# Forming the z projection of a hybrid encoder layer as seven half-size products in front of the heads

## The chip, the cores and the metric

The kernel runs on one NeuronCore of a Trainium2 chip. The metric is the device time of one execution in microseconds. Three runs of the kernel before took 2490.58, 2490.86 and 2491.49 us. Traces come from one more, profiled execution.

## What is computed

One layer for 512 tokens of width 2048, in float32. The input is RMS-normalised to h and multiplied by one wide matrix:

```python
h = rmsnorm(x, g_pre)
qkv, z_a, b_raw, a_raw, glu_in, z_b, gate_logits = split(h @ w_in)   # 6144, 2048, 16, 16, 4096, 2048, 4096 columns
# A: gated DeltaNet over 16 heads of 128
o_a = gated_delta_chunked(q, k, v, g_log, beta)
o_a = rmsnorm(o_a, g_dn_out).reshape(B, S, 2048) * silu(z_a)
y_a = o_a @ w_br_a
# B: GLU, causal depthwise convolution of 31 taps, layer norm
u = silu(layernorm(conv31(glu(glu_in)) + b_dw)) * silu(z_b)
y_b = u @ w_br_b
gate_a, gate_b = split(sigmoid(gate_logits + b_gate))
x = x + rmsnorm((gate_a * y_a + gate_b * y_b) @ w_out, g_post)
x = x + rmsnorm(sigmoid(x @ w_ple_gate) * (p @ w_ple_proj), g_ple)
```

The change concerns z_a (called z below), z_b (zb) and the two gates. For z, h is a 512 x 2048 matrix and its weight a 2048 x 2048 one.

## The kernel before, in words

**Products.** Every operand of a large product is split into a high part in the rounded type fp32r and a low remainder, and three matmuls (high-high, high-low, low-high) accumulate in a PSUM bank. `hT` holds h transposed, channels on partitions, as 16 pairs of 128x512 tiles, written at L261 (ScalarE, high) and L262 (VectorE, low). `gemm_cm` (L168) makes one output tile of 128 channels by 512 tokens from one 128-column slice of a weight: 16 k-tiles x 3 matmuls of 128x128 by 128x512 (L181, L183, L185), 48 in all. Its weights come as two loads of 512 KB into `raw` (three buffers, L121 and L122). Each load gives two pieces, and a piece is split by a ScalarE copy (L127) and a VectorE subtraction (L128) into one of four `ring` buffers. Three pieces are kept ready ahead of TensorE (L131); a piece serves 12 matmuls.

**Order.** Tiles are queued as `jobs` and run in order. `tick` (L142) counts matmuls: after every matmul each active generator comes one nearer to its next step. So the heads (`group`, a step every 4 matmuls, L664), the depthwise convolutions (every 6), the layer norm (every 10, L867) and the mixing of the branches (every 6) are issued between the matmuls of the tiles. `finish` (L152) issues what is left of a generator at once. The framework that builds the program derives the waits from the data, and gives each engine an order of its own from dependencies, free buffers and the place in the program.

**Stages.** `load_x` (L223) loads x, makes the embedding product and hT. The beta and decay tile (L267) follows, then for each of eight pairs of heads six tiles for k, q and v, the start of `group(g)`, and two tiles for z (L665): z is evacuated by a Silu with channels on partitions (`evac_z`, L438) and kept in the pool `za`. `head_scan` (L445) ends with the RMS scale (L497), a transpose of the head's output by TensorE (L502) and a multiply by g_dn_out and z (L510), once z is there (L504). Then four gate_a tiles and a GLU pair finish the heads; branch A's product runs with the other gate_a tiles, 15 GLU pairs and, on GpSimd's queue, sums of blocks of `w_out` made by accumulating loads (`presum`, L759). The gates (`evac_gate`, L712, a Sigmoid) stay in SBUF, as `mixed` and `gate_b`. The layer norm (L806) runs beside the 16 zb tiles (L869, `evac_zb`, a Silu) and the first two gate_b tiles, and ends in a Silu of its own (L848). Branch B's 16 tiles run with the other 14 gate_b tiles (L952).

**The output product** (from L998) is already made as seven half-size products in place of eight, for each half of its columns, with tokens on partitions: the stationary operands are sums and differences of quarters of the transposed activations (A11, S1 to S4), the moving ones blocks of the weight or their sums. The output's quarters are combined from the products by VectorE. The embedding gate's product follows.

**Buffers.** `slots` (L92) is a pool of 21 tiles of 128x512, shared by nearly all passing data; `lop` and `s2` (L731) hold branch B's; `gps` has two PSUM banks.

Of the kernel before, what the change touches and what calls it, by code (L numbers as in the profile page):

```python
# [9 lines left out]
F32 = mybir.dt.float32  # L10
# [5 lines left out]
P = 128  # L16
# [66 lines left out]
def _body(ctx, tc, A, out):  # L83
# [26 lines left out]
    def vv(col, n=1):  # L110
        return vec[:, col:col + n]
# [27 lines left out]
    def spawn(gen, period, key=None):  # L139
        active.append([gen, period, period, key])  # L140
# [24 lines left out]
    def w_in_tile(t):  # L165
        return A["w_in"][t]
# [56 lines left out]
    def load_x():  # L223
        with tc.tile_pool(name="xin", bufs=1) as xin, tc.tile_pool(name="xps", bufs=6, space=PSUM) as xps:
# [3 lines left out]
            prep_src.extend(ba_src)  # L228
# [209 lines left out]
    def evac_z(h):  # L438
        def f(ps):
            z = hd.tile([P, T], F32, tag="za", name="za", bufs=3)  # L440
            nc.scalar.activation(z, ps, AF.Silu)
            hstate[h].update(z=z)
        return f

    def head_scan(g, hh, G):  # L445
# [4 lines left out]
        O = hd.tile([P, NTT, P], F32, tag="O", name="O", bufs=2)  # L450
        S = None
# [44 lines left out]
        for tt in range(NTT):  # L496
            nc.vector.tensor_scalar(O[:, tt, :], O[:, tt, :], rs2[:, tt:tt + 1], None, ALU.mult)  # L497
# [6 lines left out]
        while "z" not in st:  # L504
            yield
        oa = slots.tile([P, T], F32, tag="s", name="oa")
        oav = oa.rearrange("p (t x i) -> p t x i", x=2, i=64)
        zv = st["z"].rearrange("p (t x i) -> p t x i", x=2, i=64)
        for x in range(2):
            nc.vector.scalar_tensor_tensor(oav[:, :, x, :], po[:, :, 1 - x, :], vv(V_GDN), zv[:, :, x, :], ALU.mult, ALU.mult)  # L510
# [201 lines left out]
    def evac_gate(dst, i, col, pool=None):  # L712
        def f(ps):
            gt = (pool or slots).tile([P, T], F32, tag="s2" if pool else "s", name="gt")
            nc.scalar.activation(gt, ps, AF.Sigmoid, bias=vv(V_BG + col))
            dst[i] = gt
        return f

    def gate_a(i):
        gemm_cm(w_in_tile(GATE_TILE0 + i), hT, evac_gate(mixed, i, i))  # L720

    for i in range(4):
        gate_a(i)
# [31 lines left out]
    B11, B12, B22, B21 = range(4)  # L755
# [32 lines left out]
    gate_a(4)  # L788
    glu_pair(1)
    jobs.append(lambda: finish("oa"))  # L790
    jobs.append(lambda: spawn(presum(), 10, "presum"))
    nglu = 2
    for i in range(NK):
        gemm_cm(A["w_br_a"][i], oT, evac_ya(i))
        if i + 5 < NK:
            gate_a(i + 5)
        if nglu < NK:
            glu_pair(nglu)
            nglu += 1
# [6 lines left out]
    def layer_norm():  # L806
# [36 lines left out]
        nc.scalar.copy(rstd, prs)  # L843
        yield
        for i in range(NK):
            u = u_t[i]
            nc.vector.tensor_tensor(u, u, rstd, ALU.mult)
            nc.scalar.activation(u, u, AF.Silu, scale=vv(V_LNG + i), bias=vv(V_LNB + i))  # L848
            yield
            while zb[i] is None:  # L850
                yield
# [8 lines left out]
    def evac_zb(i):  # L860
        def f(ps):
            z = low(0, "zb", F32)
            nc.scalar.activation(z, ps, AF.Silu)
            zb[i] = z
        return f
# [21 lines left out]
    LO, HI = slice(0, 256), slice(256, 512)  # L887
# [54 lines left out]
    AHEAD = 5  # L942

    def gate_b_tile(i, pool):
        gemm_cm(w_in_tile(GATE_TILE0 + 16 + i), hT, evac_gate(gate_b, i, 16 + i, pool))

    gate_b_tile(order[0], None)
    gate_b_tile(order[1], None)
    jobs.append(finish)
    for n in range(2, AHEAD):  # L950
        gate_b_tile(order[n], s2)
    for n, i in enumerate(order):  # L952
        if n + AHEAD < NK:
            gate_b_tile(order[n + AHEAD], s2)
        elif n + AHEAD == NK:
            jobs.append(lambda: spawn(mix, 6, "mix"))
        gemm_cm(A["w_br_b"][i], uT, evac_yb(i))
# [7 lines left out]

# [32 lines left out]
    OPND = {"P1": "A11", "Q5": "S1", "P7": "S3", "P6": "S2", "P3": "S4", "P2": "A12", "Q4": "A22"}  # L998
# [143 lines left out]

    def stepper(gen, n=1):
        def f(k=None):
            for _ in range(n):
                next(gen, None)
        return f
# [220 lines left out]
```

## Time and profile before

| what | value |
|---|---|
| median of three runs | 2490.86 us |
| the profiled execution | 2490.88 us |
| its span, first to last instruction | 2489.1 us |
| TensorE busy | 2469.3 us (99%) |
| VectorE busy | 1639.5 us (66%) |
| ScalarE busy | 1055.6 us (42%) |
| GpSimd busy | 230.8 us (9%) |
| granted TensorE clock, mean | 0.999 of full |
| moved by DMA | 319.32 MB, mean 128 GB/s |

PE is TensorE's matmuls and PEld its weight loads, DVE is VectorE, ACT is ScalarE, POOL is GpSimd, SP is the engine that issues most DMAs; a q behind a name is that engine's instruction queue. L181 is line 181 of the kernel. `out<-in` names the tiles that an instruction writes and reads. Busy time adds up the durations of instructions, which overlap in part on TensorE and VectorE. A time in square brackets behind an instruction is how long its engine had been idle, and what released it.

### The profile page before, as it was taken

The page shows a single profiled execution, that of the slowest core. Times are in us where ns is not written, and L with a number is a line of the kernel's source. Part 1 is how long each engine was busy: PE and PEld are TensorE (multiplying, and loading weights), DVE is VectorE, ACT ScalarE, POOL GpSimd, SP SyncE. Part 2 cuts the span into 40 slices and gives each one's busy share as a digit, 9 for nine tenths or more (in the row PEclk, how much of TensorE's full clock was granted, in tenths as well). Part 3 has the DMA queues.
Part 4 walks back from the last instruction along what each step waited for, and adds up shares of the span by engine and source line. Part 5 has one row for each costly group of instructions (what it writes and reads, how often), then busy time and mean ns, then how long its engine had stood idle before and what let it go on. Part 6 is the DMA issues. An engine that isn't in the chain of part 4 may idle for free.

```text
span 2489.1 us, 32807 instructions
## 1 busy us (share of the span) xinstructions
PE 2469.3 (99%) x12202; PEld 2037.7 (82%) x12202; DVE 1639.5 (66%) x3076; ACT 1055.6 (42%) x2083; POOL 230.8 (9%) x295
## 2 busy tenths in 40 slices
PE   9999999999999999999999999999999999999998
PEld 7888888888888888888888888887888888788886
DVE  6776767767676776887786869937423336667644
ACT  6555455565645555322222222235422224444532
POOL 0100000000000001313313200012000000000000
PEclk9999999999999999999999999999999999999999
DMA  7322222222122223857848632432232232664642
GB/s 262 119 94 73 90 76 84 83 77 90 64 94 81 77 90 93 241 157 199 220 141 224 194 110 98 155 117 95 95 101 94 95 101 94 212 235 162 202 169 77
DMA packets 101728, 319.32 MB, mean 128 GB/s; under 512 B 11968, under 2 KB 12224, under 8 KB 101568
## 3 DMA queue, kind: packets, MB, share of 16 engines
q1 hardware_dynamic: 83520, 273.18, 33.0%
q0 software_dynamic: 16896, 41.95, 6.9%
q10 hardware_dynamic: 1152, 2.10, 0.3%
q8 instruction: 95, 1.56, 0.3%
q14 instruction: 65, 0.53, 0.1%
HBM read 285.73 MB, written 31.46 MB: 127 GB/s over the span
## 4 chain that ended last, share of the span: by engine, by line
PE 97%; DVE 1%; issue 1%; ACT 0%; POOL 0%; DMA 0%; SPq 0%; DVEq 0%; POOLq 0%; ACTq 0%
PE g L183 26%; PE g L185 26%; PE g L181 25%; PE f L1052 2%; PE f L1053 2%; PE f L1051 2%; PE f L1223 2%; PE f L1222 2%; PE f L1221 2%; PE psB L467 1%; PE psS L473 1%; PE psA L461 1%; PE pg L568 1%; PE f L1300 0%; PE f L1298 0%
## 5 line engine op out<-in xcount | busy, mean ns | idle before, releaser
L185 PE MATMUL g<-hh,w 128*128 128x512 f32 x2320 | 914.9, 394 | 1.6 <-DVE w L128 1.6
L183 PE MATMUL g<-hl,w 128*128 128x512 f32 x2320 | 915.5, 395 | 0.0
L181 PE MATMUL g<-hh,w 128*128 128x512 f32 x2320 | 912.8, 393 | 0.0
L127 ACT CAST w<-raw 128x512 fp32r<-128x512 f32 x780 | 478.3, 619 | 862.8 <-PE g L185 761.5
L128 DVE TENSOR_TENSOR w<-raw,w 128x512 fp32r<-128x512 f32 x780 | 552.0, 712 | 433.7 <-ACT w L127 431.8
L185 PEld LDWEIGHTS g<-hh,w 128*128 128x128 f32 x2320 | 436.2, 188 | 88.9 <-DVE w L128 4.7
L183 PEld LDWEIGHTS g<-hl,w 128*128 128x128 f32 x2320 | 436.1, 188 | 86.8 <-issue 1.6
L181 PEld LDWEIGHTS g<-hh,w 128*128 128x128 f32 x2320 | 436.3, 188 | 84.4 <-issue 0.2
L688 DVE SCALAR_TENSOR_TENSOR uc<-sg,vec,uc 128x511 f32<-128x511 f32 (+14 forms) x480 | 351.3, 734 | 14.0 <-ACT uc L685 3.9
L409 DVE SCALAR_TENSOR_TENSOR cv<-g,vec,cv 128x511 f32<-128x511 f32 x144 | 106.5, 740 | 31.2 <-ACT cv L407 30.8
L181 PE MATMUL g<-oh,w 128*128 128x512 f32 x256 | 99.6, 389 | 0.0
L183 PE MATMUL g<-ol,w 128*128 128x512 f32 x256 | 99.6, 389 | 0.0
L185 PE MATMUL g<-oh,w 128*128 128x512 f32 x256 | 99.6, 389 | 0.0
L181 PE MATMUL g<-uh,w 128*128 128x512 f32 x256 | 99.6, 389 | 0.0
L183 PE MATMUL g<-ul,w 128*128 128x512 f32 x256 | 99.6, 389 | 0.0
L185 PE MATMUL g<-uh,w 128*128 128x512 f32 x256 | 99.6, 389 | 0.0
L603 DVE TENSOR_TENSOR prod<-UT,VT 128x2 f32<-128x2 f32 (+30 forms) x248 | 87.3, 352 | 6.6
L767 POOL DMA_DIRECT2D wsum<-in_w_out x96 | 75.2, 839 | 72.1 <-issue 22.3
L1052 PE MATMUL f<-wsp,oph 128*128 128x512 f32 x192 | 75.4, 393 | 0.1
L1051 PE MATMUL f<-wsp,oph 128*128 128x512 f32 x192 | 75.5, 394 | 0.0
L1221 PE MATMUL f<-w,xh 128*128 128x512 f32 x192 | 75.4, 393 | 0.0
L1053 PE MATMUL f<-wsp,opl 128*128 128x512 f32 x192 | 75.2, 392 | 0.0
(303 smaller groups left out, 2742.3 us busy)
## 6 DMA issues: line engine op xcount, KB each, us to landing
raw<-in_w_in SPq DMA_DIRECT2D x290, 512.0 KB, 3.3
wsum<-in_w_out POOLq DMA_DIRECT2D x96, 256.0 KB, 5.3
raw<-in_w_ple_gate SPq DMA_DIRECT2D x40, 512.0 KB, 3.4
raw<-in_w_br_a SPq DMA_DIRECT2D x32, 512.0 KB, 3.7
wo_sums<-wsum POOLq DMA_DIRECT2D x64, 256.0 KB, 3.9
raw<-in_w_br_b SPq DMA_DIRECT2D x32, 512.0 KB, 3.3
rw<-wo_sums SPq DMA_DIRECT2D x20, 512.0 KB, 4.1
rw<-in_w_out SPq DMA_DIRECT2D x13, 512.0 KB, 5.0
```

The costliest lines, as they stand in the source:

```text
L127: nc.scalar.copy(hi, rq)
L128: nc.vector.tensor_tensor(lo, rq, hi.bitcast(F32), ALU.subtract)
L181: mm(ps, wh, rh, start=(k == 0), stop=False)
L183: mm(ps, wh, rl, start=False, stop=False)
L185: mm(ps, wl, rh, start=False, stop=(k == NK - 1))
L409: nc.vector.scalar_tensor_tensor(y[:, s:], ps[:, 0:T - s], vv(w0 + 3 - s), y[:, s:], ALU.mult, ALU.add)
L603: pin(nc.vector.tensor_tensor(pv_, um, vm, ALU.mult))
L688: nc.vector.scalar_tensor_tensor(y[:, s:], u[:, 0:T - s], vv(w0 + TAPS - 1 - s), y[:, s:], ALU.mult, ALU.add)
L1051: mm(ps, lh, wh[:, c], start=kk == 0, stop=False)
L1052: mm(ps, lh, wl[:, c], start=False, stop=False)
L1053: mm(ps, ll, wh[:, c], start=False, stop=kk == 7)
L1221: mm(ps[tt], lh, wh, start=k == 0, stop=False)
```

## The change

The z tiles between the heads go. In front of the heads there is a new phase, `z_phase`. Four gate tiles (`FILL`) run first, and beside them, every 4 matmuls, a step of `form`: it adds hT's high and low parts and builds and splits S1 to S4. Then, for each of the two halves of z's columns (`jp`), three runs of products: P1 and Q5, then P6, P7 and P3, then P2 and Q4. Each product has four quarters q of the k range with two weight pieces of 128x512 each; a piece serves 6 matmuls. Blocks of the z weight are loaded in pieces of 512 KB, 3 of 5 into `raw`, 2 of 5 into slots; T1 (B11 + B12) and B12 + B22 are formed by VectorE, and T2 and T4 by accumulating loads on GpSimd's queue onto T1 (B22, then B21). The results have tokens on partitions; a Silu on ScalarE and two stores put each into DRAM, by head, with the halves of 64 tokens swapped as the heads hold them. `head_scan` loads its z, multiplies it in at the RMS scale, and the evacuation of the transpose becomes a ScalarE copy scaled by g_dn_out.

All other gate tiles and the zb tiles are made in the places that are free (`rest`, in the order gate_a 4 to 15, zb 0 to 15, gate_b 0 to 15): two behind each pair of heads, five around the first two GLU pairs, eleven in branch A's product, and the last twelve beside the layer norm. Each is stored to DRAM and loaded again three tiles ahead of its use. The layer norm's period goes from 10 to 8 matmuls; the mixing is spawned with a period of 10 before the seventh tile of branch B, instead of 6 before the twelfth. The beta tile comes behind the z phase.

```diff
-    ba_src = [w_in_tile(BA_TILE)[0], w_in_tile(BA_TILE)[1]]
+    z_dram = dram.tile([NH, P, NTT, P], F32, name="z_dram")
+    g_dram = dram.tile([2 * NK, P, T], F32, name="g_dram")
+    zb_dram = dram.tile([NK, P, T], F32, name="zb_dram")
+    def gate_tile(i, src=True):
+        def f(ps):
+            t = slots.tile([P, T], F32, tag="s", name="gt")
+            nc.scalar.activation(t, ps, AF.Sigmoid, bias=vv(V_BG + i))
+            nc.sync.dma_start(g_dram[i], t)
+        gemm_cm(w_in_tile(GATE_TILE0 + i) if src else None, hT, f)
...
     load_x()
-    gemm_cm(None, hT, lambda ps: spawn(beta_decay(ps), 5))
+    def z_phase():
+        ctx_z = ExitStack()
+        zs = ctx_z.enter_context(tc.tile_pool(name="zs", bufs=32))
+        zps = ctx_z.enter_context(tc.tile_pool(name="zps", bufs=6, space=PSUM))
...
+        def form():
+            for k2 in range(4):
+                hf = {}
+                for k in (2 * k2, 2 * k2 + 8, 2 * k2 + 1, 2 * k2 + 9):
+                    hf[k] = slots.tile([P, T], F32, tag="s", name="hf")
+                    tt_(hf[k], hT[k][0].bitcast(F32), hT[k][1].bitcast(F32), ALU.add)
+                    yield
...
+                for kk, c in both:
+                    tt_(s1[:, c], hf[kk][:, HI], hf[kk + 8][:, HI], ALU.subtract)
+                split_s("S1", k2, s1)
+                yield
...
+        def load(jp, blk, q):
+            cnt["load"] += 1
+            if cnt["load"] % 5 in (2, 4):
+                two = [slots.tile([P, T], F32, tag="s", name="zraw") for _ in range(2)]
+                for n in range(2):
+                    nc.sync.dma_start(two[n], WZ[jp, blk, q][:, n * T:(n + 1) * T])
+                return two
+            raw = rawp.tile([P, 1024], F32, tag="raw", name="raw", bufs=3)
+            nc.sync.dma_start(raw, WZ[jp, blk, q])
+            return [raw[:, 0:T], raw[:, T:]]
+        def acc(t, jp, blk, q):
+            nc.gpsimd.dma_start(t, WZ[jp, blk, q], accum_op=ALU.add)
...
+        def e_a(jp, q):
+            b11, b12 = load(jp, B11, q), load(jp, B12, q)
+            tz[q] = zs.tile([P, 1024], F32, tag="t", name="zt", bufs=4)
+            t = parts(tz[q])
+            for n in range(2):
+                tt_(t[n], b11[n], b12[n], ALU.add)
+            return [b11, t]
+        def e_b(jp, q):
+            acc(tz[q], jp, B22, q)
+            b22, b12 = load(jp, B22, q), load(jp, B12, q)
+            for n in range(2):
+                tt_(b12[n], b12[n], b22[n], ALU.add)
+            return [parts(tz[q]), b12, b22]
+        def e_c(jp, q):
+            acc(tz[q], jp, B21, q)
+            return [load(jp, B21, q), parts(tz[q])]
+        for jp in range(2):
+            for e in (e_a, e_b, e_c):
+                entries.extend((e, jp, q) for q in range(4))
+        def piece():
+            while len(pieces) < 4 and (sources or entries):
+                while len(sources) < 4 and entries:
+                    e, jp, q = entries.popleft()
+                    for src in e(jp, q):
+                        sources.extend(src)
+                src = sources.popleft()
...
+                nc.scalar.copy(hi, src)
+                tt_(lo, src, hi.bitcast(F32), ALU.subtract)
+                pieces.append((hi, lo))
+            return pieces.popleft()
+        def run(products, side=None):
+            ps = {pr: [zps.tile([P, T], F32, tag="z", name="zp") for _ in range(2)] for pr in products}
+            for q in range(4):
+                for pr in products:
+                    for n in range(2):
+                        wh, wl = piece()
+                        for t in range(2):
+                            lh, ll = opnd(OPND[pr], 2 * q + n, t)
+                            mm(ps[pr][t], lh, wh, start=q + n == 0, stop=False)
+                            mm(ps[pr][t], lh, wl, start=False, stop=False)
+                            mm(ps[pr][t], ll, wh, start=False, stop=q == 3 and n == 1)
...
+        def fin(tt, j, c):
+            nc.scalar.activation(c, c, AF.Silu)
+            cv = c.rearrange("p (h d) -> p h d", d=P)
+            for a in (0, 64):
+                nc.sync.dma_start(z_dram[4 * j:4 * j + 4, 64 - a:128 - a, tt, :].rearrange("h p d -> p h d"), cv[a:a + 64])
+        gen = form()
+        gate_tile(0, False)
+        for i in range(1, FILL):
+            gate_tile(i)
+        spawn(gen, 4, "form")
+        run_jobs()
+        for jp in range(2):
+            ps = run(("P1", "Q5"), stepper(gen, 2))
+            s1, s5 = [], []
+            for home, pr in ((s1, "P1"), (s5, "Q5")):
+                for t in range(2):
+                    home.append(unit_s("zsn"))
+                    nc.scalar.copy(home[t], ps[pr][t])
+            ps = run(("P6", "P7", "P3"))
...
+            ps = run(("P2", "Q4"))
...
+        finish("form")
+        ctx_z.close()
+    FILL = 4
+    z_phase()
+    gemm_cm(w_in_tile(BA_TILE), hT, lambda ps: spawn(beta_decay(ps), 5))
...
+        z = hd.tile([P, NTT, P], F32, tag="za", name="za", bufs=3)
+        nc.sync.dma_start(z, z_dram[h])
...
-            nc.vector.tensor_scalar(O[:, tt, :], O[:, tt, :], rs2[:, tt:tt + 1], None, ALU.mult)
+            nc.vector.scalar_tensor_tensor(O[:, tt, :], O[:, tt, :], rs2[:, tt:tt + 1], z[:, tt, :], ALU.mult, ALU.mult)
...
-            nc.vector.scalar_tensor_tensor(oav[:, :, x, :], po[:, :, 1 - x, :], vv(V_GDN), zv[:, :, x, :], ALU.mult, ALU.mult)
+            nc.scalar.activation(oav[:, :, x, :], po[:, :, 1 - x, :], AF.Copy, scale=vv(V_GDN))
...
+    rest = deque([lambda i=i: gate_tile(i) for i in range(FILL, NK)] + [lambda i=i: zb_tile(i) for i in range(NK)]
+                 + [lambda i=i: gate_tile(NK + i) for i in range(NK)])
...
-        for h in pair:
-            gemm_cm(w_in_tile(Z_TILE0 + h), hT, evac_z(h))
+        for _ in range(2):
+            rest.popleft()()
...
-    jobs.append(lambda: spawn(layer_norm(), 10))
-    for i in range(NK):
-        gemm_cm(w_in_tile(ZB_TILE0 + i), hT, evac_zb(i))
+    jobs.append(lambda: spawn(layer_norm(), 8))
+    while rest:
+        rest.popleft()()
```

## Rows read from the trace of the kernel before

**Rows 1.** Page, busy time: engine, busy us (share of the span), instructions.

```profile
PE 2469.3 (99%) x12202; PEld 2037.7 (82%) x12202; DVE 1639.5 (66%) x3076; ACT 1055.6 (42%) x2083; POOL 230.8 (9%) x295
```

**Rows 2.** Page, the chain that ended last, shares by engine.

```profile
PE 97%; DVE 1%; issue 1%; ACT 0%; POOL 0%; DMA 0%; SPq 0%; DVEq 0%; POOLq 0%; ACTq 0%
```

**Rows 3.** Waits of TensorE: who waited for whom, us in total, times, longest.

```profile
PE e_ps L213 <- ACT w L127: 6.1, 1, 6.1
PE g L185 <- DVE w L128: 1.6, 2, 1.3
PE f L1135 <- DVE snap L1129: 0.7, 1, 0.7
...
PE pv L555 <- ACT junk L551: 0.3, 1, 0.3
```

**Rows 4.** Timeline, ScalarE, two gate evacuations: start us, us, engine, line, operation.

```profile
1036.60 0.69 ACT L715 ACTIVATE gt<-g,vec 128x512 f32<-128x512 f32 x1 [2.10 <-PE g L185]
...
1080.12 0.69 ACT L715 ACTIVATE gt<-g,vec 128x512 f32<-128x512 f32 x1 [2.10 <-PE g L185]
```

**Rows 5.** Timeline, VectorE, operations back to back.

```profile
43.38 2.49 DVE L128 TENSOR_TENSOR w<-raw,w 128x512 fp32r<-128x512 f32 x4
...
2146.40 0.76 DVE L918 TENSOR_TENSOR sf<-sf,gt 128x256 f32<-128x256 f32 x2
```

**Rows 6.** Timeline, first matmul of the first tile, and its evacuation.

```profile
36.03 0.48 PE L181 MATMUL g<-hh,w 128*128 128x512 f32 x1
...
50.43 0.57 ACT L298 COPY ba_cm<-g 32x512 f32<-32x512 f32 x1
```

**Rows 7.** Windows: stretch, us, busy PE, PEld, DVE, ACT, POOL; clock, DMA share, GB/s.

```profile
2150.00:2250.00 100.00, 99.68 (x434) 81.48 (x435) 62.43 (x66) 51.46 (x66) 0.00 (x0) 1.00 0.72 247
1000.00:1250.00 250.00, 250.00 (x1105) 207.01 (x1104) 202.22 (x297) 69.97 (x113) 69.03 (x96) 1.00 0.72 201
```

**Rows 8.** DMA issues: operation, count, KB each, median us from issue to landing.

```profile
raw<-in_w_in SPq DMA_DIRECT2D x290, 512.0 KB, 3.3
wsum<-in_w_out POOLq DMA_DIRECT2D x96, 256.0 KB, 5.3
```

**Rows 9.** Timeline, GpSimd, near the start.

```profile
0.81 0.52 POOL L286 MEMSET Tc<- 128x512 f32 x1
...
10.48 0.55 POOL L247 TENSOR_TENSOR xrs<-xms,mhalf_c 128x1 f32<-128x1 f32 x1 [7.12 <-DVE xms L245]
```

**Rows 10.** Groups by line and shape, VectorE: count, busy us, mean ns, idle before.

```profile
L510 DVE SCALAR_TENSOR_TENSOR oa<-po,vec,za 128x256 f32<-128x256 f32 x32 | 13.3, 478 | 1.5 <-PE po L502 0.9
```

**Rows 11.** Timeline, ScalarE, table loads; last row: who waited for L715.

```profile
65.42 1.28 ACT L418 ACT_TABLE_LOAD   x1 [0.70 <-DVE cv L409]
...
67.37 1.28 ACT L361 ACT_TABLE_LOAD   x1
68.66 0.28 ACT L361 ACTIVATE eS<-gc_ps 128x128 f32<-128x128 f32 x1
...
126.95 1.28 ACT L434 ACT_TABLE_LOAD   x1
...
910.98 1.28 ACT L715 ACT_TABLE_LOAD   x1
...
1622.04 1.28 ACT L863 ACT_TABLE_LOAD   x1
...
  PEld pd L639: 0.4, 1
```

**Rows 12.** Timeline, layer norm: a weight split on VectorE, and TensorE's wait.

```profile
1676.08 1.78 DVE L128 TENSOR_TENSOR w<-raw,w 128x512 fp32r<-128x512 f32 x1
...
1688.33 0.50 PE L185 MATMUL g<-hh,w 128*128 128x512 f32 x1 [0.33 <-DVE w L128]
```

More of the change, by code (lines that the diff above doesn't have):

```diff
@@ L227, in load_x @@
             prep_src.extend(A["w_ple_proj"][j] for j in range(4))
-            prep_src.extend(ba_src)
+            prep_src.extend(first_src)
             pT = embed_in()
@@ new lines, in zb_tile, with f @@
+    def zb_tile(i):
+        def f(ps):
+            t = slots.tile([P, T], F32, tag="s", name="zb")
+            nc.scalar.activation(t, ps, AF.Silu)
+            nc.sync.dma_start(zb_dram[i], t)
+        gemm_cm(w_in_tile(ZB_TILE0 + i), hT, f)
+    first_src = [w_in_tile(GATE_TILE0)[0], w_in_tile(GATE_TILE0)[1]]
+    load_x()
+    LO, HI = slice(0, 256), slice(256, 512)
+    B11, B12, B22, B21 = range(4)
+    OPND = {"P1": "A11", "Q5": "S1", "P7": "S3", "P6": "S2", "P3": "S4", "P2": "A12", "Q4": "A22"}
@@ L436, in evac_v @@
         return f
[L438 to L443, printed above, removed]
     def head_scan(g, hh, G):
@@ L503, in head_scan @@
         yield
-        while "z" not in st:
-            yield
         oa = slots.tile([P, T], F32, tag="s", name="oa")
         oav = oa.rearrange("p (t x i) -> p t x i", x=2, i=64)
-        zv = st["z"].rearrange("p (t x i) -> p t x i", x=2, i=64)
         for x in range(2):
-            nc.vector.scalar_tensor_tensor(oav[:, :, x, :], po[:, :, 1 - x, :], vv(V_GDN), zv[:, :, x, :], ALU.mult, ALU.mult)
+            nc.scalar.activation(oav[:, :, x, :], po[:, :, 1 - x, :], AF.Copy, scale=vv(V_GDN))
         o_a[h] = oa
@@ L710, in _body @@
     gate_b = [None] * NK
[L712 to L720, printed above, removed]
     for i in range(4):
-        gate_a(i)
+        rest.popleft()()
     glu_pair(0)
@@ L754, in _body @@
     WO = A["w_out"]
-    B11, B12, B22, B21 = range(4)
     T1, T2, T3, T4 = range(4)
@@ L786, in presum, with load_gate @@
                 yield from give(a, T4)
-    gate_a(4)
+    def load_gate(i):
+        mixed[i] = slots.tile([P, T], F32, tag="s", name="gt")
+        nc.sync.dma_start(mixed[i], g_dram[i])
+    rest.popleft()()
     glu_pair(1)
     jobs.append(lambda: finish("oa"))
+    for i in range(3):
+        jobs.append(lambda i=i: load_gate(i))
     jobs.append(lambda: spawn(presum(), 10, "presum"))
@@ L794, in _body @@
         gemm_cm(A["w_br_a"][i], oT, evac_ya(i))
+        if i + 3 < NK:
+            jobs.append(lambda i=i: load_gate(i + 3))
         if i + 5 < NK:
-            gate_a(i + 5)
+            rest.popleft()()
         if nglu < NK:
@@ L843, in layer_norm @@
         nc.scalar.copy(rstd, prs)
+        for i in range(3):
+            load_zb(i)
         yield
@@ L849, in layer_norm @@
             yield
-            while zb[i] is None:
-                yield
+            if i + 3 < NK:
+                load_zb(i + 3)
             nc.vector.tensor_tensor(u, u, zb[i], ALU.mult)
@@ L858, in layer_norm, with load_zb @@
             yield
[L860 to L865, printed above, removed]
-    jobs.append(lambda: spawn(layer_norm(), 10))
-    for i in range(NK):
-        gemm_cm(w_in_tile(ZB_TILE0 + i), hT, evac_zb(i))
+    def load_zb(i):
+        zb[i] = low(0, "zb", F32)
+        nc.sync.dma_start(zb[i], zb_dram[i])
+    jobs.append(lambda: spawn(layer_norm(), 8))
+    while rest:
+        rest.popleft()()
     mixT = [None] * NK
@@ L886, in _body @@
     Sf = {}
-    LO, HI = slice(0, 256), slice(256, 512)
     def sw_split(pool, tag, src):
@@ L940, in _body, with load_gate_b @@
     order = [k + 8 * n for k in range(8) for n in range(2)]
[L942 to L948, printed above, removed]
+    def load_gate_b(i):
+        gate_b[i] = s2.tile([P, T], F32, tag="s2", name="gb")
+        nc.sync.dma_start(gate_b[i], g_dram[NK + i])
     jobs.append(finish)
-    for n in range(2, AHEAD):
-        gate_b_tile(order[n], s2)
+    for n in range(3):
+        jobs.append(lambda n=n: load_gate_b(order[n]))
     for n, i in enumerate(order):
[L953 to L956, printed above, removed]
+        if n + 3 < NK:
+            jobs.append(lambda n=n: load_gate_b(order[n + 3]))
+        if n == 6:
+            jobs.append(lambda: spawn(mix, 10, "mix"))
         gemm_cm(A["w_br_b"][i], uT, evac_yb(i))
@@ L1141, in post @@
                 yield
[L1143 to L1147, printed above, removed]
     def drain(gen):
@@ L1347 @@
         "w_in": _cm_tiles(w_in, cols),
+        "w_z": _sw_tiles(w_in[:, Z_TILE0 * P:(Z_TILE0 + NH) * P]),
         "w_br_a": _cm_tiles(a["w_br_a"], [c * P for c in range(NK)]),
```

69 lines of the change are left out of this document (68 added, 1 removed).

## The prediction

> **What bounds the kernel now.** I read the busy shares first, then the chain, then TensorE's own waits. TensorE is busy for 2469.3 of 2489.1 us while VectorE has 66% and ScalarE 42% [rows 1], and 97% of the chain that ended last is TensorE [rows 2]. In the whole span its waits on another engine are 6.1 us once at the start and 1.6 us for late weight pieces, with nothing else over 0.7 us [rows 3]. So a matmul removed is time removed, and any engine may take what it likes as long as TensorE is never left without operands. The profiled execution took 2490.88 us, 1.8 us more than its span; the median of the runs is 2490.86 us, so sums against the one hold for the other.
>
> A matmul's price is its step, not its duration. In the records matmuls overlap. Two gate evacuations, four tiles (4 x 48 = 192 matmuls) apart, lie 43.52 us apart [rows 4]: 0.2267 us each.
>
> **What goes.** Before, z costs 16 tiles x 48 = 768 matmuls of 128x128x512. After, each column half has 7 products of 8 k-tiles x 2 token tiles x 3 split terms = 48 matmuls: 2 x 7 x 48 = 672, same shape. 96 fewer: **-21.8 us**. Nothing else on TensorE changes in number: gates and zb are 48 tiles before and after, and they take z's places between the heads, so the heads get the same 64 tiles to hide in.
>
> **The fill in front of z.** The first four gate tiles give TensorE work while VectorE forms the sums of hT. Per k2 that is 8 operations of 512 columns and 8 of 256: 32 + 32 in all. Four 512-column subtractions in a row take 2.49 us, the last one 0.69, so the step is 0.60; two of 256 take 0.76, a step of 0.34 [rows 5]. 32 x 0.60 + 32 x 0.34 = 30.1 us, and 14 weight splits of these tiles add 8.4. VectorE is taken by the hl casts until 43.38, where these subtractions begin [rows 5], so it is through at 43.4 + 38.5 = 81.9. The 32 steps of the forming are issued every 4 matmuls, over 128 matmuls. The first tile's matmuls run from 36.03 to about 50.4 [rows 6], the remaining 80 take 18.1 us to 68.5, and three pieces split ahead cover 36 matmuls or 8.2 us: 76.7. VectorE is 5.2 us late: **+5 us**. Bounds: nothing, if the splits are placed ahead of the forming; 12 us, if every operation costs its full duration (0.69 and 0.42) instead of its step. I take 5, from the steps seen back to back.
>
> **The z phase itself.** 672 x 0.2267 = 152 us. A weight piece is now used up by 6 matmuls instead of 12, one every 1.36 us. VectorE: 112 splits and 32 block sums at 0.60, and 28 combinations of products at about 0.63 = 104 us, 68% of the phase. ScalarE: 112 copies, 8 evacuations and 16 silus at about 0.6 = 82 us. Neither is the bound. DMA: 40 loads and 16 accumulating loads of 512 KB are 29.4 MB, and 16 z tiles of 256 KB 4.2 MB: 33.6 MB in 152 us, 221 GB/s. The nearest stretch is the output product, which has the same shape: 247 GB/s over 100 us with TensorE idle for 0.32 us [rows 7]. The branch-A stretch, which holds such accumulating loads, moved 201 GB/s without an idle moment, at a DMA share of 0.72 [rows 7]. No row shows a store in pieces of 512 B as z's are, nor an accumulating load of 512 KB; the nearest, a plain load of 512 KB and an accumulating one of 256 KB, land in 3.3 and 5.3 us [rows 8]. Bounds for waits in this phase: zero, as in the branch-A stretch, and 15 us, if 201 GB/s were all there is (33.6 MB / 201 = 167 us). I take **+3 us**, nearer the output product, for the four ends of runs, where eight stores and a string of combinations come at once.
>
> Entering and leaving it, z's first loads stand in program order behind a gate's store, which waits for TensorE; so does beta's first load behind z's last stores. Were SP's order the program's, each would cost a landing (3.3 us [rows 8]), a copy and a subtraction, some 5 us. But the queues are not in program order: the memset of L286 ran at 0.81 us, ahead of the power of L247 at 10.48 on the same engine [rows 9]. I expect loads to move ahead as buffers come free: zero, with up to 10 us in the range.
>
> **The heads.** Per head, two multiplies of 128x256 on VectorE (478 ns [rows 10]) become two scaled copies on ScalarE, and the four scalings become multiplies with z in token layout; z comes by one 256 KB load, issued at the head's start, tens of microseconds ahead of its use. The chain is not longer. Each tile's store (256 KB) joins SP behind an evacuation; the raw loads it may hold up have three buffers, six pieces or 16 us, of cover. Priced at nothing.
>
> What is new is the activation table. Sigmoid and Silu sit in different tables: a load stands before the first Sigmoid after Silus at 910.98, one before the first Silu after it [rows 11]. Counting the new order: 12 switches from six pairs of gates in the heads, some 17 from zb tiles among the glu pairs, some 10 from the late gates inside the layer norm: about 39, against 3 after the heads' start. 36 x 1.28 = 46 us more of ScalarE, which has over 1400 idle. The one switch of before inside a head held a weight load of TensorE up by 0.4 us [rows 11]. In the heads the gate tiles fall where VectorE solves the triangle. Zero, bounded by 12 x 0.4 = 5 us if each costs what that one did.
>
> The Trainium skill ("ScalarE: Activation LUTs", What ACT_TABLE_LOAD costs) puts a switch at 1.28 us plus a drain of 1.38, about 2.66 us, and says to batch calls by table, which this change undoes. By that price the 36 would take 96 us of ScalarE. The trace agrees on the 1.28 but shows no drain: the Exp starts 0.01 us behind its load [rows 11].
>
> **The layer norm.** It lost 6 of the 18 tiles that it ran beside. It has 69 steps after some 11 of waiting for the last depthwise convolution: 80 steps every 8 matmuls are 640, and there are 12 x 48 = 576. Eight steps, four channels, are issued after the last tile: 4 x 3 VectorE operations, 7.2 us, while branch B's first tile reaches its 13th operand after 36 matmuls, 8.2 us. Also, while VectorE and GpSimd share the mean's subtraction, a split takes 1.78 us instead of 0.69, and TensorE waits 0.33 us even now [rows 12]; the shorter period leaves less cover. **+2 us**, bounds 0 and 6 (the 1.6 us of late pieces [rows 3] doubled, and 3 for the four channels). Gates come back by 256 KB loads three tiles ahead, over 30 us: nothing.
>
> **Sum.** 2490.9 - 21.8 + 5 + 3 + 2 = **2479.1 us**.
>
> **The rivals.** (a) All of it is hidden: 2469.1 us. For it speak the output product and branch-A stretches; against it the 38.5 us of VectorE work in the fill. (b) The z phase runs at what DMA gives, 201 GB/s: 15 us instead of 3, with 5 and 2 as before: 2491.1, no change. For it: the densest sustained stretch with accumulating loads shows no more. Against it: 247 GB/s in the output product, at the same share 0.72. (c) Slower: table switches become TensorE waits. A Silu or a copy of a weight piece behind an unexpected load holds the head's next small matmul, which stands in TensorE's order in front of the tiles. If all 36 cost their 1.28 us, 46 us on top of the sum: 2525. It decides from (21.8 - 10 + 5) / 1.28 = 13 exposed switches on, where the time passes 2496. Against it: 0.4 us for the one seen, and eleven switches between 65.42 and 126.95 us, among beta's work and the first heads [rows 11], with which TensorE's only wait was 0.3 us [rows 3]. By the skill's 2.66 us per switch the same rival would give 2575, and seven exposed switches would do.
>
> **Chances.** The forecast, with waits of 5 to 15 us given back: 0.5. (a) 0.2. (b) 0.18, of which a little lands faster or slower than its 0.2%. (c) and other ways to slower, 0.12. About 0.2% (5 us) is what a measurement here can tell from no change. Faster 0.71, same 0.17, slower 0.12. Range: 2468.5, (a) with its rounding, to 2491.5, (b); beyond it lies (c).
>
> **What would show it.** Right: TensorE's matmul count down by 96; a wait on VectorE's splits between 60 and 90 us of about 5 us; z's 672 matmuls in some 155 us; heads without idle time; one short wait before branch B. Wrong: TensorE waiting for DMA loads in z (b), waits for ScalarE in the heads (c), or a wait of over 4 us at z's first or last matmul, which would mean that SP kept program order after all.

## The result, and the profile after

The changed kernel takes 2499.8 us (median of 6 runs, 2498.61 to 2500.66) against 2491.28 us of the kernel before, timed beside it (6 runs, 2490.58 to 2492.53). The ratio is 1.0034, 95% interval 1.0021 to 1.0047: slower, where 2479.1 us and faster were forecast, and outside the range. The profiled execution took 2499.71 us with a span of 2497.9 us, 8.8 us above the span of before.

The page of the kernel after, the busy times and the chain that ended last:

```profile
PE 2461.0 (99%) x12106; PEld 2021.4 (81%) x12106; DVE 1728.1 (69%) x3216; ACT 1151.5 (46%) x2223; POOL 243.2 (10%) x311
...
PE 91%; DVE 3%; ACT 2%; issue 2%; DMA 1%; SPq 0%; POOL 0%; DVEq 0%; POOLq 0%; ACTq 0%
```

Beside [rows 1, 2]: the 96 matmuls are gone (12202 to 12106), and yet the span grew. TensorE's idle time went from 19.8 us (2489.1 - 2469.3) to 36.9 (2497.9 - 2461.0), and 6 points of the chain moved from TensorE to other engines. The waits of TensorE after, in the columns of [rows 3], say for whom:

```profile
PE g L185 <- DVE w L128: 6.4, 9, 2.9
PE e_ps L213 <- ACT w L127: 6.1, 1, 6.1
PE g L181 <- ACT w L127: 5.4, 7, 0.9
PE zp L425 <- ACT w L412: 3.2, 3, 2.5
PE zp L426 <- DVE w L311: 2.2, 3, 1.4
PE g L181 <- ACT gt L272: 0.8, 1, 0.8
```

The second line was there before; the other five are new or grown. They name VectorE and ScalarE, and the weight pieces of the gate tiles (`g`) as well as those of z (`zp`).

To see where the time went, the span is cut at four events that both kernels have. Timeline of after: the beta tile's evacuation, the last tile of branch A (L944) and the first of branch B (L1075):

```profile
264.69 0.57 ACT L508 COPY ba_cm<-g 32x512 f32<-32x512 f32 x1
...
1837.50 0.68 DVE L944 TENSOR_TENSOR gt<-g,gt 128x512 f32<-128x512 f32 x1
...
1986.13 0.69 DVE L1075 TENSOR_TENSOR gb<-g,gb 128x512 f32<-128x512 f32 x1 [1.38 <-PE g L185]
```

Between the first two lie the transposes of the heads' outputs, one line with its count, its durations and its first and last start:

```profile
L707 PE MATMUL po<-cst,O x24: 272/273/273, 988.6 to 1204.5; 128*128 128x128 f32 x24
```

The same of before, by line (the beta tile's is in [rows 6]):

```profile
L502 PE MATMUL po<-cst,O x8: 272/272/273, 980.2 to 981.0; 128*128 128x128 f32 x8
...
L750 DVE TENSOR_TENSOR gt<-g,gt x2: 683/683/683, 1603.0 to 1614.0; 128x512 f32<-128x512 f32 x2
L875 DVE TENSOR_TENSOR gt<-g,gt x7: 691/692/693, 1868.5 to 1999.0; 128x512 f32<-128x512 f32 x7
```

| stretch | before, us | tiles moved, at 10.88 us and 0.2267 a matmul | so expected | after, us | lost |
|---|---|---|---|---|---|
| start to beta's evacuation | 50.4 | + 4 gates + 672 matmuls of z | 246.2 | 264.7 | 18.5 |
| to the heads' last transpose | 930.6 | the same number | 930.6 | 939.8 | 9.2 |
| to branch A's last tile | 633.0 | the same number | 633.0 | 633.0 | 0 |
| to branch B's first tile | 254.5 | 10 tiles less | 145.7 | 148.6 | 2.9 |
| to the end | 620.6 | 10 tiles less | 511.8 | 511.8 | 0 |

The losses are 30.6 us; -21.8 + 30.6 = +8.8 us, the difference of the spans. In the first stretch the fourth gate is evacuated at 89.47 us, where 50.4 + 3 x 10.88 = 83.1 would be full rate: 6.4 us were lost in the fill and 12.0 in z. Of the 6.4, 0.7 lie ahead of the fill: its first matmul starts at 36.77 us, that of before at 36.03 [rows 6], and in the experiments made from after, none of which changes what comes before it, between 35.84 and 37.30. So four places carry the result: the fill, z's beginning, the heads and the layer norm.

**The fill.** Timeline of TensorE, kernel after:

```profile
57.41 0.50 PE L181 MATMUL g<-hh,w 128*128 128x512 f32 x1 [0.78 <-ACT gt L272]
...
77.28 0.80 PE L185 MATMUL g<-hh,w 128*128 128x512 f32 x1 [2.95 <-DVE w L128]
77.87 0.63 PE L181 MATMUL g<-hh,w 128*128 128x512 f32 x1
78.29 0.63 PE L183 MATMUL g<-hl,w 128*128 128x512 f32 x1
```

The forecast wait on VectorE's splits is there, 2.95 us at the forecast place. But it costs more than it lasts: behind it the steps are 0.42 us instead of 0.23 until 80. The window of that stretch (columns as in [rows 7]) shows the clock:

```profile
78.00:80.00 2.00, 2.00 (x7) 1.54 (x5) 2.00 (x6) 0.54 (x1) 0.00 (x0) 0.50 0.61 102
```

The granted clock is 0.50, the lower of the two levels (1.2 GHz), after TensorE had stood for 2.95 us. That adds some 1.4 us (from 77.28 to 80.00, six steps in 2.72 us instead of 1.36). It does not happen each time. In the experiments x2 and x6 below, whose edits lie behind the fill, the same wait leaves the clock at full speed; here x2:

```profile
77.68 0.50 PE L185 MATMUL g<-hh,w 128*128 128x512 f32 x1 [2.95 <-DVE w L128]
...
78.00:80.00 2.00, 2.00 (x10) 1.64 (x9) 2.00 (x6) 0.39 (x2) 0.00 (x0) 1.00 0.41 78
```

From the fill's first matmul to the fourth gate's evacuation these two take 51.3 us, after 52.7: the same 1.4 us. Why the clock fell in one run and not in the other, no row shows.

**The beginning of z.** TensorE, and then SP's queue:

```profile
96.09 0.73 PE L425 MATMUL zp<-w,zoh 128*128 128x512 f32 x2 [2.54 <-ACT w L412]
...
115.77 0.50 PE L426 MATMUL zp<-w,hh 128*128 128x512 f32 x1 [1.42 <-DVE w L311]
```

```profile
82.03 0.37 SPq L364 DMA_DIRECT2D zraw<-in_w_z  x1
90.18 0.33 SPq L273 DMA_DIRECT2D g_dram<-gt  x1
90.57 1.39 SPq L364 DMA_DIRECT2D zraw<-in_w_z  x3
```

SP issued nothing between 82.40 and 90.18: it stood at the store of the fourth gate, which could not go before that gate's evacuation at 89.47 to 90.16, and three loads of z came right behind it. The waits at 111 to 116 have another face. DMA issues of 60 to 125 us, and the window of the waits:

```profile
zt<-in_w_z POOLq DMA_DIRECT2D x5, 512.0 KB, 8.6
```

```profile
100.00:120.00 20.00, 17.68 (x71) 13.29 (x71) 10.94 (x18) 8.07 (x15) 3.48 (x4) 0.98 0.92 239
160.00:250.00 90.00, 90.00 (x391) 73.15 (x390) 60.55 (x96) 45.30 (x79) 9.95 (x19) 1.00 0.78 215
```

There the DMA engines are busy for 0.92 of the time, and an accumulating load of 512 KB takes 8.6 us to land. Once past it, z never waits: 391 matmuls in 90 us. That is 0.2302 us each, though, not 0.2267: 672 of them are 2.4 us more, a part of the 12.0. The larger part is lost early: in the 30.7 us from z's first matmul (89.27) to 120 TensorE does 97 of z's matmuls, where 133 would fit at 0.2302, a loss of 8.4 us. Some 1.4 of these (an estimate) are again the clock, 0.50 and 0.80 in the windows of 98 to 100 and 100 to 102 us, behind the wait of 2.54. 8.4 and 2.4 leave 1.2 of the 12.0 that these rows do not place.

**The heads.** ScalarE, the third pair of heads' gate tile:

```profile
350.90 8.17 ACT L788 COPY Ud<-W 32x1024 f32<-32x1024 f32 x4 [2.50 <-DVE W L774]
359.08 1.28 ACT L272 ACT_TABLE_LOAD   x1
360.38 0.69 ACT L272 ACTIVATE gt<-g,vec 128x512 f32<-128x512 f32 x1
360.96 2.17 ACT L127 CAST w<-raw 128x512 fp32r<-128x512 f32 x4
```

and TensorE at the same time:

```profile
360.37 0.39 PE L185 MATMUL g<-hh,w 128*128 128x512 f32 x1
361.62 0.50 PE L181 MATMUL g<-hh,w 128*128 128x512 f32 x1 [0.86 <-ACT w L127]
...
362.56 0.50 PE L185 MATMUL g<-hh,w 128*128 128x512 f32 x1 [0.21 <-DVE w L128]
```

The copies of the triangle (`Ud`) hold ScalarE for 8.2 us. The three pieces kept ready are 36 matmuls, 8.2 us: just enough. The table load stands between them and the next weight copies, and TensorE runs dry. From 360.37 to 361.62 is 1.25 us, 1.0 over a step, and the second wait adds 0.4. The same pair of waits stands at six places between 361 and 908 us, 109 us apart, one in each pair of heads with gate tiles, and 6 x 1.5 = 9 us is the loss of that stretch.

**The layer norm.** GpSimd's subtractions, in a row, and on VectorE a weight split beside them, on TensorE the wait:

```profile
1889.14 8.60 POOL L1021 TENSOR_TENSOR ur<-ur,mean 128x512 f32<-128x512 f32 x5 [41.70 <-DVE mean L1017]
...
1891.41 1.78 DVE L128 TENSOR_TENSOR w<-raw,w 128x512 fp32r<-128x512 f32 x1
...
1909.34 0.50 PE L185 MATMUL g<-hh,w 128*128 128x512 f32 x1 [1.59 <-DVE w L128]
```

These are the rows of [rows 12] again, with a wait of 1.59 us where there was one of 0.33 (and one of 1.3, [rows 3]).

### The profile page after: what moved, and what is told of

Same layout as the page of the kernel before. It is cut to its first block, busy times and chain, and to the rows that moved or that the text cites. A ratio compares the mean times of both kernels' runs of the same rounds, so it can differ in the third digit from the quotient of the medians.

```text
span 2497.9 us, 33218 instructions
## 1 busy us (share of the span) xinstructions
PE 2461.0 (99%) x12106; PEld 2021.4 (81%) x12106; DVE 1728.1 (69%) x3216; ACT 1151.5 (46%) x2223; POOL 243.2 (10%) x311
## 4 chain that ended last, share of the span: by engine, by line
PE 91%; DVE 3%; ACT 2%; issue 2%; DMA 1%; SPq 0%; POOL 0%; DVEq 0%; POOLq 0%; ACTq 0%
PE g L185 22%; PE g L183 22%; PE g L181 22%; PE zp L425 2%; PE zp L426 2%; PE zp L427 2%; PE f L1241 2%; PE f L1242 2%; PE f L1404 2%; PE f L1405 2%; PE f L1240 2%; PE f L1406 2%; ACT Ud L788 1%; PE psB L672 1%; PE psS L678 1%
## 5 line engine op out<-in xcount | busy, mean ns | idle before, releaser
L185 PE MATMUL g<-hh,w 128*128 128x512 f32 x2064 | 817.0, 396 | 6.4 <-DVE w L128 6.4
L181 PE MATMUL g<-hh,w 128*128 128x512 f32 x2064 | 815.8, 395 | 6.1 <-ACT w L127 5.4
L183 PE MATMUL g<-hl,w 128*128 128x512 f32 x2064 | 816.7, 396 | 0.0
L127 ACT CAST w<-raw 128x512 fp32r<-128x512 f32 x716 | 439.1, 619 | 749.6 <-PE g L185 635.0
L128 DVE TENSOR_TENSOR w<-raw,w 128x512 fp32r<-128x512 f32 x716 | 505.4, 710 | 285.8 <-ACT w L127 283.9
L185 PEld LDWEIGHTS g<-hh,w 128*128 128x128 f32 x2064 | 388.9, 188 | 86.3 <-DVE w L128 11.9
L181 PEld LDWEIGHTS g<-hh,w 128*128 128x128 f32 x2064 | 389.1, 189 | 83.9 <-ACT w L127 8.3
L183 PEld LDWEIGHTS g<-hl,w 128*128 128x128 f32 x2064 | 388.6, 188 | 76.7 <-issue 1.6
```

What stands on the lines that cost most here:

```text
L127: nc.scalar.copy(hi, rq)
L128: nc.vector.tensor_tensor(lo, rq, hi.bitcast(F32), ALU.subtract)
L181: mm(ps, wh, rh, start=(k == 0), stop=False)
L183: mm(ps, wh, rl, start=False, stop=False)
L185: mm(ps, wl, rh, start=False, stop=(k == NK - 1))
```

## The experiments

All but one are made from the kernel after, most by a single edit. "Beta" is the start of the beta tile's evacuation (264.7 us after). A time without a number of runs is that of a single run. Medians of the kernel before beside them were 2490.94, 2491.26 and 2491.58 us in the three series.

**x1_zb_first: no table switch in the heads.** zb tiles, evacuated by a Silu as much else there, come first, the gates later.

```diff
-    rest = deque([lambda i=i: gate_tile(i) for i in range(FILL, NK)] + [lambda i=i: zb_tile(i) for i in range(NK)]
+    rest = deque([lambda i=i: zb_tile(i) for i in range(NK)] + [lambda i=i: gate_tile(i) for i in range(FILL, NK)]
```

> Only the order of the tiles in the free places changes: zb 0 to 15 first, then gate_a 4 to 15, then gate_b, so that the sixteen tiles between the heads are evacuated by Silu, as the heads' own tiles are. Same stores, same loads, same matmuls. Theory (table loads): in the changed kernel each of the six pairs of heads with gate tiles is 109.0 us apart instead of 107.5, because a table load of 1.28 us stands on ScalarE behind the 8.2 us copy and in front of the weight copies; then the pairs come back to 107.5 us, the stretch from the beta tile's evacuation to the last transpose of a head goes from 939.8 us to some 931, and the whole to about 2491 us. Rival (the store on SP and the longer way of the tile are what costs, whatever the function): the stretch stays at some 940 us and the whole at 2500 us.

2491.22 us (10 runs; ratio to before 1.000, 0.9991 to 1.001), 8.6 less than after. Beta is unchanged at 264.6, and from there to the last transpose (1195.4) are 930.8 us, the 930.6 of before. ScalarE at the place shown above:

```profile
350.81 8.17 ACT L788 COPY Ud<-W 32x1024 f32<-32x1024 f32 x4 [2.50 <-DVE W L774]
359.00 0.60 ACT L279 ACTIVATE zb<-g 128x512 f32<-128x512 f32 x1
```

The same copies, the same evacuation, the load alone is missing, and TensorE's waits there with it. The heads' loss is the table loads, and all of it.

**x2_t2_vector: B22 added by VectorE instead of an accumulating load.**

```diff
-            acc(tz[q], jp, B22, q)
...
+                tt_(parts(tz[q])[n], parts(tz[q])[n], b22[n], ALU.add)
```

> The eight accumulating loads that add B22 to T1 go; VectorE adds the B22 that is loaded anyway (16 subtractions' worth, about 10 us of VectorE in the z phase, which has 30% idle). 4.2 MB less is moved. Theory (the early accumulating loads take the DMA engines from the loads that z's next pieces wait for, from 98 to 116 us): the waits of TensorE between 108 and 117 us go, and the beta tile's evacuation comes about 5 us earlier than 264.7. Rival (the late start of z's loads behind the last gate's store is all of z's loss): the evacuation stays within 2 us of 264.7, or comes later for VectorE's extra work.

2495.57 us, beta 260.2 (-4.5). Of the 4.5, 1.0 is the fill, where nothing was changed: the fourth gate is evacuated at 88.44 instead of 89.47, with the full clock shown above. From there to beta it is 171.8 us instead of 175.2, a gain of 3.5. The waits at 111 to 116 are gone, though VectorE has 16 more operations; the one of 2.6 us at 95 stays:

```profile
80.00:100.00 20.00, 16.87 (x67) 13.07 (x66) 12.77 (x23) 7.72 (x14) 0.00 (x0) 0.92 0.54 174
100.00:120.00 20.00, 20.00 (x88) 16.20 (x87) 15.47 (x25) 10.34 (x18) 1.08 (x1) 1.00 0.65 203
```

**x3_act_store: the first four gates' stores on ScalarE's queue.**

```diff
-            nc.sync.dma_start(g_dram[i], t)
+            (nc.scalar if i < FILL else nc.sync).dma_start(g_dram[i], t)
```

> The stores of the first four gate tiles are issued from ScalarE's queue instead of SP's, so that z's first loads on SP no longer stand behind a store that waits for TensorE. Theory (SP's order holds z's loads back: between 82.4 and 90.2 us SP waited for the fourth gate): z's second quarter is loaded some 8 us earlier, the wait of 2.5 us at 96 us and part of those at 111 to 116 us go, and the beta tile's evacuation comes 4 to 8 us earlier than 264.7. Rival (z's loss is DMA contention and VectorE): within 2 us of 264.7.

2500.46 us, beta 265.7 (+1.0): no gain. But the wait did go; it came back later, in the windows:

```profile
80.00:100.00 20.00, 20.00 (x88) 16.40 (x88) 13.98 (x24) 8.52 (x15) 2.38 (x3) 1.00 0.63 193
100.00:120.00 20.00, 16.43 (x56) 12.08 (x55) 8.02 (x13) 7.45 (x14) 2.18 (x3) 0.83 0.90 232
```

From 80 to 100 TensorE is fully busy. From 100 to 120 it does 56 matmuls instead of 71, at a granted clock of 0.83: z's loads come earlier, GpSimd's accumulating loads go out 4.5 us earlier (93.59 instead of 98.14), and the DMA engines saturate as before (share 0.90). Up to 120 us x3 is still a little ahead of after. The +1.0 comes from two waits late in z that after does not have, some 2.7 us together:

```profile
206.84 0.50 PE L426 MATMUL zp<-w,zoh 128*128 128x512 f32 x1 [0.74 <-DVE w L311]
...
216.80 0.50 PE L426 MATMUL zp<-w,zoh 128*128 128x512 f32 x1 [1.37 <-DVE w L311]
```

x1, whose z phase is that of after, has one of 0.87 us there (215.61), so beta scatters by such waits from run to run. VectorE stood for late loads there (5.8 and 2.2 us in x3); what makes them late was not tested. For the first waits, either the two stand in series, and removing the first only feeds the second, or the store matters little. That asked for both edits together.

**x7_store_t2: x2 and x3 together.**

> The edits of x2 and x3 together. Alone, the store edit moved the beta tile's evacuation by +1.0 us and the VectorE edit by -4.5 us. Theory (two waits in a row, for late loads and then for loads beside the early accumulating ones, each of which takes the other's place): together they give more than their sum, the evacuation comes 7 to 10 us earlier than 264.7. Rival (independent): 3 to 5 us earlier.

2492.12 us, beta 257.0: -7.7, where the two alone add up to -3.5. z's own matmuls between 89 and 120 us leave out the fill and the late waits; the windows of after, x2, x3 and x7, for the tile `zp` alone:

```profile
89.00:120.00 31.00, 25.35 (x97) 19.01 (x98) 0.00 (x0) 1.78 (x4) 0.94 0.77 208
89.00:120.00 31.00, 27.87 (x114) 21.83 (x113) 0.00 (x0) 2.35 (x4) 0.94 0.63 197
89.00:120.00 31.00, 27.43 (x103) 21.05 (x103) 0.00 (x0) 2.35 (x4) 0.89 0.76 198
89.00:120.00 31.00, 30.53 (x132) 24.71 (x133) 0.00 (x0) 2.35 (x4) 1.00 0.60 189
```

(Here the columns behind the two of TensorE are VectorE and ScalarE.) Adding on VectorE gains 17 matmuls, moving the stores 6, both together 35. In series, then: with the second wait gone, moving the stores gives 18 matmuls, some 4 us (171.8 to 167.5 from the fourth gate to beta), that it did not give alone. z has no wait on a piece left in the view of waits; of its loss 4.3 us remain, 2.4 of them the longer step.

**x5_plain_loads: is it the adding, or the bytes?** GpSimd's 16 loads overwrite instead of adding. The sums T2 and T4 are thereby left out, with the same loads, bytes and order.

```diff
-            nc.gpsimd.dma_start(t, WZ[jp, blk, q], accum_op=ALU.add)
+            nc.gpsimd.dma_start(t, WZ[jp, blk, q])
```

> GpSimd's sixteen loads onto T1 overwrite instead of accumulating, so that the sums T2 and T4 are left out; bytes read, queue, sizes and waits stay. Theory (adding in the DMA makes such a load take the DMA engines for longer than its bytes do): the DMA share between 98 and 116 us falls, TensorE's waits between 108 and 117 us shrink, and the beta tile's evacuation comes 3 to 5 us earlier than 264.7. Rival (it is the bytes and their early time on a second queue): the evacuation stays within 1.5 us of 264.7.

2496.63 us, beta 261.9 (-2.8, just short of the 3 expected; from the fourth gate 172.0 us instead of 175.2, -3.2). The loads land in 5.9 us instead of 8.6 (the first five), and 292 GB/s are moved where it was 239, TensorE fully busy:

```profile
100.00:120.00 20.00, 20.00 (x84) 16.02 (x84) 12.76 (x21) 10.49 (x19) 2.16 (x4) 0.95 0.85 292
```

GpSimd's queue from 60 to 125 us, in after and here (packets, MB, the time that its packets took as a share of the 16 DMA engines):

```profile
q0 software_dynamic: 673, 2.49, 20.8%
q0 software_dynamic: 720, 2.62, 11.1%
```

For about the same bytes the adding loads keep the DMA engines busy nearly twice as long. So most of what x2 gained in z (3.2 of 3.5) is the adding inside the DMA, which takes DMA time that plain loads of the same bytes do not. Single runs scatter by about 1 us, so the shares are rough.

**x4_form_6: the sums of hT formed every 6 matmuls instead of 4.**

```diff
-        spawn(gen, 4, "form")
+        spawn(gen, 6, "form")
```

> The forming of the sums takes a step every 6 matmuls instead of every 4: the same work spread over the whole of the four gate tiles. Theory (VectorE's order puts forming ahead of weight splits and so makes TensorE wait 3 us at 74 us, plus what the fallen clock costs): the waits before 80 us go, the fourth gate's evacuation comes some 5 us earlier than 89.5, and the work left over is done behind z's first pieces. Rival (VectorE's amount of work sets the end, whatever its order): TensorE's wait moves to z's first pieces, and the beta tile's evacuation stays within 2 us of 264.7.

2493.45 us, beta 258.5 (-6.2). The fourth gate is evacuated at 82.82 us, which is full rate, and the window from 60 to 80, 17.05 us busy in after, is full:

```profile
60.00:80.00 20.00, 20.00 (x90) 16.58 (x89) 19.54 (x40) 9.97 (x17) 0.00 (x0) 1.00 0.40 138
```

VectorE is as full as it was (19.5 of 20 us). It does the splits in time and the forming later, where z's first products can still take it. The fill's loss was one of order.

**y_all: x1, x2, x3 and x4 together.**

> The edits of x1, x2, x3 and x4 together: zb tiles first, B22 added by VectorE, the first four gates stored from ScalarE's queue, forming every 6 matmuls. Theory (four separate losses: table loads 9 us, the order of forming 6 us, the late loads and the early accumulating loads together up to 12 us): the beta tile's evacuation at 247 to 252 us, the heads' stretch at 931 us, the whole at 2474 to 2479 us, faster than the kernel before by 12 to 17 us. Rival (the z phase has a floor of its own by VectorE or DMA): the evacuation stays above 255 us and the whole above 2482 us.

2478.81 us (5 runs; ratio to before 0.9950, 0.9937 to 0.9964): faster than both kernels. Beta 251.4, and 931.1 us of heads.

**x6_ln_vector: all subtractions of the mean on VectorE.**

```diff
-            (nc.gpsimd if i % 3 == 2 else nc.vector).tensor_tensor(u, u, mean, ALU.subtract)
+            nc.vector.tensor_tensor(u, u, mean, ALU.subtract)
```

> In the layer norm the five subtractions of the mean that GpSimd does (1.75 us each) go to VectorE (0.6 us each). Theory (while GpSimd and VectorE both work, VectorE's operations take 1.7 us instead of 0.7, and this burst, with the shorter period, makes TensorE wait for weight splits): the waits of 0.6, 0.3 and 1.6 us between 1900 and 1910 us go, and the stretch from the last evacuation of branch A to the first of branch B goes from 148.6 us to 146. Rival (the shorter period alone leaves VectorE too much to do): the stretch stays or grows, as VectorE gets 3 us more.

2494.6 us; from branch A's last tile to branch B's first 144.5 us (1836.4 to 1980.9) instead of 148.6. VectorE got five operations more, and yet of the late splits one of 0.5 us is left.

**b_ln_vector: the same edit in the kernel before** (there L820).

> The kernel before with this one edit, all mean subtractions of the layer norm on VectorE. If the layer norm's loss was there before the change and the change only lost cover for it, the kernel before gains its 1.6 us of late weight pieces and up to the 4.3 us by which the stretch from the last branch-A to the first branch-B evacuation (254.5 us) exceeds 23 tiles of 10.88: 250 to 252 us there, and a time of 2487 to 2489. Rival: the loss is the change's own (shorter period, fewer tiles beside it), and the kernel before stays within 0.5 us of 2491, with 254 us in the stretch.

2489.83 us (10 runs; ratio to before 0.9993, 0.9984 to 1.0002, which can't be told from no change); the stretch takes 252.3 us (1615.0 to 1867.3) instead of 254.5, and no wait on a piece is left in it. So 2.2 of the 4.1 us were there before the change, by one profile of each kernel, and 1.9 came with it. Whether these come from the shorter period or from the fewer tiles was not tried.

**z_best: y_all with that edit.**

> The version with zb first, gate stores on ScalarE's queue, B22 added by VectorE and the forming every 6 matmuls, and now also all mean subtractions of the layer norm on VectorE. If the stretches are independent, as my accounting takes them to be, the 4.1 us that this edit gave by itself come off 2478.8: 2474.7 us, last branch-A to first branch-B evacuation 144.5 us. Rival: the zb tiles no longer lie beside the layer norm (gate_b tiles do), there are no table switches between tiles there, and less is to be had: 2477 to 2478, and 146 to 148 us.

2475.15 us (2474.12 to 2475.59, 5 runs; ratio to before 0.9934, 0.9921 to 0.9948), 24.6 less than the change as it was made. The stretch is 144.6 us (1815.7 to 1960.3). (The rival's premise does not hold: gate_b tiles and table loads lie beside the layer norm in after, too.) All that TensorE still waits for in the four places, in the view of waits, but for one of 0.4 us in the heads that was there before (L555 in [rows 3]):

```profile
PE zp L425 <- ACT zw L412: 1.5, 1, 1.5
...
PE g L185 <- DVE w L128: 0.5, 1, 0.5
```

Beta is at 251.6: of the first stretch's 18.5 us, 5.4 are left, 2.4 of them the longer step.

## Why the prediction was wrong, point by point

**What bounds it, and what goes: right, but for the size of a step.** TensorE's matmuls fell by 96, and full-rate stretches run as forecast. The price 0.2267 came from gate tiles, which are a different product. z's step is 0.2302, and the row that showed it was at hand: the output product, 434 matmuls in 99.68 us, 0.230 each [rows 7]. 768 x 0.2267 - 672 x 0.2302 = 19.4 us, not 21.8; below, the 2.4 are counted in z.

**The fill, +5: right place, right engine, 6.4 us.** The lateness of VectorE by 5.2 us had been worked out from its steps. The wait was 2.95 us, and some 1.4 came from the granted clock behind it; 0.8 was a third tile held by a late evacuation, and 0.7 lay ahead of the first matmul. So that 5 comes near 6.4 is in part luck: the wait was little over half of what was forecast, and the rest is made of terms that were priced nowhere. The clock's 1.4 is itself a matter of the run, as x2 and x6 show.

**z, +3: 12.0, the term that was furthest off besides the heads.** Two steps failed. First, "But the queues are not in program order: [...] I expect loads to move ahead as buffers come free: zero, with up to 10 us in the range." SP stood for 7.8 us at a store with loads of z behind it. [rows 9] show an instruction placed early on GpSimd; they don't show a load passing a store that waits. The test named for it, a wait of over 4 us at z's first matmul, was not met (2.54), but the cause was the one named. Second, the DMA term. It weighed a mean of 221 GB/s over the phase against 247 and 201 of other stretches. The mean was fine (215 from 160 on, without a wait). What failed was the first 25 us, where the first loads and the accumulating ones come at once, at a share of 0.92 and 239 GB/s. The bound of 15 us held the size; the choice near the lower end leaned on the output product, whose loads are all plain. The row of 256 KB and 5.3 us [rows 8] did not show the price of adding either: by the kernel (`presum`) only 64 of its 96 loads add.

**The heads, zero: 9.2 us, the failed step.** "In the heads the gate tiles fall where VectorE solves the triangle. Zero, bounded by 12 x 0.4 = 5 us if each costs what that one did." Exactly in that place ScalarE is not free: it copies `Ud` for 8.2 us, as much as the three ready pieces cover. 0.4 us was the price of a switch with cover; without it 1.28 us of load costs 1.5. This is rival (c) in mechanism, with 6 exposed switches and not 13. The other six in the heads, back to the former table, cost nothing: without them, too, x1's heads only came back to before's length. The count of switches was nearly good: 35 table loads from the first gate in the heads on, where about 39 were forecast (12 in the heads and 17 among the GLU pairs, as counted, but 6 in the layer norm). That after has just 36 more than before is luck, as it also has four more ahead of the heads' gates. All but those six cost no time that can be seen: the stretch with the GLU pairs takes 633.0 us in both kernels, and beside the layer norm's (1932 to 1966 us) TensorE is fully busy.

The Trainium skill ("ScalarE: Activation LUTs", What ACT_TABLE_LOAD costs) puts a switch at 1.28 us plus 1.38 of drain, and further on (Table sets: the hidden batching unit) tells to batch calls by set. The batching is what x1 did, and it gave 8.6 us. The drain is not in these rows: the Sigmoid starts at 360.38, 0.02 us behind its load's end at 359.08 + 1.28.

**The layer norm, +2: 2.9, right in size.** Of the two mechanisms named for it, x6 and b_ln_vector show the shared subtraction: 1.9 us more of it than before. The other, the four late channels, shows no wait in after: TensorE is busy for all of the time from 1920 to 1986 us. 1.0 us is left, 0.5 of it the wait that stays in x6. The Trainium skill ("SBUF — State Buffer", Who interferes with whom) says that a VectorE instruction with two SBUF inputs contends with a GpSimd one that reads SBUF. The trace agrees: 1.78 us instead of 0.69 for the split, and taking GpSimd's part away shortened the stretch although VectorE does more.

**The sum.** Forecast -21.8 + 5 + 3 + 0 + 2 = -11.8; measured, in the same terms, -21.8 + 6.4 + 12.0 + 9.2 + 2.9 = +8.8 (rounded). Rival (b), z at what DMA gives, would have taken 15 us throughout; its loss is there, but in the first 25 us, and it is gone with one operand's sums on VectorE and the four stores on another queue (x7). What stays open: why z's step is 1.5% longer than a gate tile's, and how the last 3 us before beta (5.4 less 2.4) divide.

## What to carry to other kernels

When TensorE is the bound with a few pieces of lead, price a moved tile by what the engine that evacuates it is doing at that place: a table load of 1.28 us is free with cover, and costs all of itself where something else has just used the cover up. Waits at one place stand in series: an edit that removes the first may show next to nothing, as moving the stores did, until the second is gone too, so test them together before dropping either. A mean rate over a phase says little of its first 25 us, where the queues fill: read that stretch by itself, order what is issued there, and keep stores that wait out of the queue of the loads.

## What the runs showed of the hardware

- A wait of TensorE can cost more than it lasts, but does not each time. After 2.95 us the granted clock was 0.50 (1.2 GHz) in the window of 78 to 80 us of after, with steps of 0.42 us instead of 0.23; in x2 and x6 it was 1.00 there after the same wait, and the fill took 1.4 us less. In x3 the window of 100 to 120 us, with waits of 0.45 to 1.81 us, had a mean of 0.83.
- An accumulating load of 512 KB landed in 8.6 us where the same load without adding took 5.9 (median of the first five in each), at 239 GB/s against 292, and its queue's packets took 20.8% of the DMA engines' time against 11.1% for about the same bytes.
- The same matmul of 128x128x512 has a step of 0.2267 us in products with channels on partitions and 0.2302 in z's, which has tokens there (0.230 in the output product, too); the cause is open.
